# Preparing the keys of the first attention in fixed places of the input block before it

## The chip, the cores and the metric

The kernel runs on one core of one Trainium2 chip. The metric is the device time of one execution in microseconds (us). Beside the times of several runs there is one profiled execution with a trace of every instruction. Engines are named as the profile names them: PE multiplies matrices (PEld loads its weights), DVE, ACT and POOL compute on vectors, SP only issues transfers. Each engine takes its own instructions strictly in the order in which they stand in its queue, and waits where an operand is not ready.

## The reference

One encoder layer on a sequence of 512 tokens of width 2048, in float32. What the change touches is the input projection and the start of mixer A:

```python
h = rmsnorm(x, g_mix)
qa, ka, va, qb, kb, vb = split(h @ w_in)
q = axial_rope(rmsnorm(qa, g_q), s) * hd ** -0.5    # 8 heads of 128
k = axial_rope(rmsnorm(ka, g_k), s)                 # 2 heads of 128
p = softmax(q @ k.T);  out_a = p @ va               # all 512 keys
```

Mixer B (dilated windows), the output projection, a SwiGLU layer and a last norm follow; they are the same in both kernels.

## The kernel before

**Products.** Every float32 operand is split into a high and a low part, and a product is three matmuls (`mm3`, lines 242 to 244): high by high, high by low, low by high. For each tile of weights ACT makes the high part (line 295, in the attention stage) and DVE the low part (line 300); line 271 is its load, issued by SP.

**Units.** The program is a list of units, each one weight tile with its matmuls. The input projection has a first chunk of 16 units (keys and values of mixer A, parked in DRAM as `kvA`), three blocks of 56 column units that use seven products in place of eight (`ColBlock`, products m1 to m7, in the order of `CHAIN`, m3 last), and then two plain chunks of 16 units (`in_plain`), whose units have 12 matmuls each. The queries of mixer A, `qA0` and `qA1`, are made in the first of the three blocks and parked in DRAM too. The last of the three blocks, `last`, is where the change is; its results (the first queries and keys of mixer B) are evicted by lines 939 and 944.

**Pieces between units.** After the matmuls of unit n the program runs the functions hooked to n. `last.after("m3", k, f)` hooks f to the unit k places behind the last m3 unit of the block, so -4 is four units before its end. Besides, `side` is a queue of small pieces of attention work. `give` hands out a credit, 2.8 for each unit in the attention stage (half of it in the middle of the unit, half at its end), and runs pieces from the front of `side` while the credit covers their cost; a piece costs 1 unless `weighed`, `light` or `both` gives it another cost. So neither a clock nor readiness sets the order: it is written out when the program is built, and an engine that comes to a piece whose operand is late stands still, with everything queued behind it.

**The start of the attention.** `load_consts` loads the gains and the rotary tables `ctab`. `reload("kvA", kA)` brings the keys and values back from DRAM, 1 MB in one transfer. `table_tasks` makes six pieces: three for the keys' tables `gsk` and `gck` (lines 420 and 414) and three for the queries' `gsq`, `gcq`. Then, for each of four row tiles t: `scale_k` (ACT, line 501) with the squares of the keys (ACT, line 435, tile `rj`); `split_vA` (ACT line 497, DVE line 498); the squares of the queries with the turned and scaled keys (DVE, lines 448 to 458); the turned and scaled queries (DVE, the same lines on `qA`). A norm's root is taken on POOL after a small DVE instruction (line 222). The keys are transposed by PE (line 506), the queries of the first head by `heads[0].tq` (line 550), which needs all four scaled row tiles; then the slots of the heads begin.

The queue and its start are:

```python
todo = attention_tasks()
last.after("m3", 0, lambda: side.extend(todo))
last.after("m3", 1, lambda: reload("kvA", kA))
last.after("m3", 2, lambda: reload("qA0", qA[0]))
```

Of the kernel before, what the change touches and what calls it, by code (L numbers as in the profile page):

```python
# [23 lines left out]
NT = S // P  # L24
KD = D // P
NC = D // 512
NHA, NKV, NHB = 8, 2, 8
# [42 lines left out]
def encoder_block(ctx, tc, x, g_mix, w_in, g_q_a, g_k_a, g_out_a, g_out_b, w_out, g_ffn,  # L70
# [15 lines left out]
    def slot(base, dtype=F32, shape=(P, 512)):  # L86
        return sp.tile(list(shape), dtype, tag="s", name=nm(base))
# [11 lines left out]
    def bank():  # L99
        return banks.popleft()  # L100

    def release(*tiles):
        banks.extend(tiles)
# [203 lines left out]
    side = deque()  # L307
# [154 lines left out]
    qA, kA, kTA, vA = {}, {}, {}, {}  # L462
# [21 lines left out]
    def reload(name, dst):  # L484
        assert stored[name] == NT, name
        whole = slot(name, F32, (P, NT, 512))
        nc.sync.dma_start(whole, spill[name].rearrange("t p c -> p t c"))
        dst.update((t, whole[:, t]) for t in range(NT))
        dst["whole"] = whole
# [10 lines left out]
    def scale_k(t):  # L500
        nc.scalar.activation(kA[t][:, :256], kA[t][:, :256], AF.Copy, scale=r1["r"][:, t:t + 1])

    def transpose_k_a(kv):
        ps = bank()
        for t in range(NT):
            nc.tensor.transpose(ps[:, t * P:(t + 1) * P], kA[t][:, 256 + kv * HD:256 + (kv + 1) * HD], ident)
        kTA[kv] = split(ps, "kT", at=((2, 4 + 2 * kv), (2, 5 + 2 * kv)))
        release(ps)
# [8 lines left out]
    def split_vB(h):  # L517
        vB[h] = split(vB[h].rearrange("p t c -> p (t c)"), "v", at=heads[NHA + h].home("v"))
# [16 lines left out]
    heads = []  # L535
# [102 lines left out]
    def push_heads():  # L638
        for n in range(2 * NHA):
            heads.append(Head("AB"[n // NHA], n % NHA))  # L640
# [20 lines left out]
    def weighed(cost, f):  # L661
        f.cost = cost
        return f

    def light(cost, tasks):
        return [weighed(cost, f) for f in tasks]

    def attention_tasks():
        def q_tasks(j):
            return norm_rope(lambda t: (qA[j][t], qA[j][t]), 4, "q")  # L670

        def both(cost, *lists):
            return [weighed(cost, lambda fs=fs: [f() for f in fs]) for fs in zip(*lists)]

        qA.update({j: {} for j in range(2)})
        qkB.update({j: {} for j in range(4)})
        push_heads()
        k_squares, k_turned, k_scaled = norm_rope(lambda t: (kA[t][:, :256], kA[t][:, 256:]), NKV, "k")
        q_squares, q_turned, q_scaled = q_tasks(0)
        vs = [lambda t=t: split_vA(t) for t in range(NT)]  # L680
        tables = light(0.8, table_tasks())
        todo = tables[:3] + both(1.4, [lambda t=t: scale_k(t) for t in range(NT)], k_squares)
        todo += both(0.6, vs) + tables[3:]
        todo += both(2.0, q_squares, k_turned, k_scaled) + both(2.6, q_turned, q_scaled)
        todo += light(0.6, [lambda kv=kv: transpose_k_a(kv) for kv in range(NKV)]) + [heads[0].tq, heads[0].tk]
        todo += light(0.1, [lambda: reload("qA1", qA[1])])
        extra = {}

        def at(slot, tasks):
            extra.setdefault(slot, []).extend(tasks)  # L690
        at(20, light(0.1, [lambda: nc.sync.dma_start(mask, c_mask)]))
        q_squares, q_turned, q_scaled = q_tasks(1)
        for t in range(NT):
            at(t // 2, both(0.8, q_squares[t:t + 1]))
            at(2 + 2 * t, both(0.9, q_turned[t:t + 1]))
            at(3 + 2 * t, both(0.9, q_scaled[t:t + 1]))
        for j in range(4):
            s = NT * (NHA + 2 * j)
            at(s - 11, light(0.1, [lambda j=j: reload(f"qkB{j}", qkB[j])]))
            at(s - 7, light(0.9, [lambda j=j: rope_partial(qkB[j]["whole"])]))  # L700
        for h in range(NHB):
            s = NT * (NHA + h)
            at(s + 2, light(0.1, [lambda h=h: load_vB(h)]))
            at(s + 4, light(0.4, [lambda h=h: split_vB(h)]))
        for s in range(2 * NHA * NT + VALUE_LAG + 2):
            cost = 1.5 if s < NHA * NT else 1.2 if s < 2 * NHA * NT else 0.7
            todo += [weighed(cost, lambda s=s: head_slot(s))] + extra.get(s, [])
        return todo

    share = {"now": -1, "credit": 0.0, "due": 1.0}  # L710

# [251 lines left out]
    blocks, ends = [], []  # L963
# [7 lines left out]
              (("qkB2", "qkB3"), heads_b[2:])]  # L971
    for names, lo in groups[:COLUMN_BLOCKS]:
        in_block(names, lo)
    last = blocks[-1]
    last.after("m7", 1, lambda: nc.gpsimd.dma_start(arena[0][:, 1], ar_dram))
    last.after("m3", -2, load_consts)
    todo = attention_tasks()
    last.after("m3", 0, lambda: side.extend(todo))
    last.after("m3", 0, twins.clear)
    last.after("m3", 0, leave_homes)  # L980
    last.after("m5", 0, lambda: fewer_homes("more"))
    last.after("m3", 1, lambda: reload("kvA", kA))
    last.after("m3", 2, lambda: reload("qA0", qA[0]))
    attend = [len(units)]
    for names, lo in groups[COLUMN_BLOCKS:]:
# [508 lines left out]
```

## Time and profile before

| what | value |
|---|---|
| time, median of 3 runs | 1978.44 us (1978.35 to 1980.0) |
| the profiled execution, its own time | 1978.67 us |
| its span in the trace | 1976.9 us |
| PE busy | 1965.3 us |
| DVE busy | 1590.2 us |
| ACT busy | 1130.4 us |

A row of the timeline has the start in us from the span's start, the length, the engine, the line, the operation and its tiles, and how often it stands in a row; in brackets the idle time of the engine before it and what ended that. A length holds the pipeline's fill, so the time that an instruction costs its engine in a row of them is the distance between two starts, a little less than its length. A row of the windows has a stretch of the span, its length, the busy time of PE, PEld, DVE, ACT and POOL in it with their instructions, PE's granted clock (1.00 is full), the share of the transfer engines and GB/s.

### The profile page before, as it was taken

How to read it: one execution, taken by the hardware profiler on the slowest of the kernel's cores; microseconds unless marked ns; L12 is line 12 of the kernel's file. 1: busy time of each engine (PE TensorE's matmuls, PEld its weight loads, DVE VectorE, ACT ScalarE, POOL GpSimd, SP SyncE). 2: the span in 40 equal slices, each digit the busy share in tenths (PEclk: the TensorE clock that was granted, in tenths of full speed). 3: DMA queues.
4: the chain of work that ended last, by engine and by line, in shares of the span. 5: the costliest groups of instructions: out<-in, count | busy, mean ns of one | idle time of the engine just before them, and what ended most of it. 6: DMA issues, size and time to landing. Idle time of an engine off the chain costs nothing.

```text
span 1976.9 us, 27536 instructions
## 1 busy us (share of the span) xinstructions
PE 1965.3 (99%) x8972; PEld 1621.9 (82%) x8972; DVE 1590.2 (80%) x2725; ACT 1130.4 (57%) x2071; POOL 120.3 (6%) x162
## 2 busy tenths in 40 slices
PE   9999999999999999999999999999999999999998
PEld 7888888888888888888888888888888888888886
DVE  6888668888775698887878877878779888878877
ACT  7655555565455565554554555555555666656655
POOL 0100001000000000000000000000000121111121
PEclk9999999999999999999999999999999999999999
DMA  8576683143343564745837747558467698879865
GB/s 279 181 282 205 216 275 126 68 144 128 118 146 104 203 208 163 280 159 193 303 115 253 243 134 279 197 179 287 142 218 267 191 275 252 226 149 264 239 128 171
DMA packets 235873, 394.83 MB, mean 200 GB/s; under 512 B 22560, under 2 KB 77648, under 8 KB 235600
## 3 DMA queue, kind: packets, MB, share of 16 engines
q1 hardware_dynamic: 211440, 330.85, 50.1%
q0 software_dynamic: 17200, 40.38, 9.4%
q10 hardware_dynamic: 7088, 21.83, 3.3%
q8 instruction: 70, 1.15, 0.2%
q14 instruction: 75, 0.61, 0.1%
HBM read 330.33 MB, written 62.65 MB: 199 GB/s over the span
## 4 chain that ended last, share of the span: by engine, by line
PE 95%; DVE 2%; DMA 1%; ACT 1%; issue 1%; SPq 0%; ACTq 0%; POOLq 0%; POOL 0%; DVEq 0%
PE b L242 31%; PE b L244 31%; PE b L243 30%; PE b L600 1%; PE b L1164 1%; DMA raw<-in_w_in_dram 1%; PE b L1088 0%; PE b L326 0%; PE b L550 0%; DVE w L300 0%; ACT rj L435 0%; DVE ra L448 0%; DMA stage<-in_w_in_dram 0%; PE b L561 0%; DVE qA L457 0%
## 5 line engine op out<-in xcount | busy, mean ns | idle before, releaser
L242 PE MATMUL b<-tw,arena 128*128 128x512 f32 x2244 | 879.3, 392 | 0.0
L244 PE MATMUL b<-tw,arena 128*128 128x512 f32 x2244 | 874.1, 390 | 0.0
L243 PE MATMUL b<-tw,arena 128*128 128x512 f32 x2244 | 873.6, 389 | 0.3 <-DVE tw L300 0.3
L828 ACT ACTIVATE tw<-raw 128x512 fp32r<-128x512 f32 x924 | 557.4, 628 | 427.3 <-DVE raw L891 290.9
L831 DVE TENSOR_TENSOR tw<-raw,tw 128x512 fp32r<-128x512 f32 x924 | 619.8, 686 | 161.9 <-ACT tw L828 155.9
L244 PEld LDWEIGHTS b<-tw,arena 128*128 128x128 f32 x2244 | 421.2, 188 | 88.2
L243 PEld LDWEIGHTS b<-tw,arena 128*128 128x128 f32 x2244 | 421.5, 188 | 86.7 <-DVE tw L300 0.6
L242 PEld LDWEIGHTS b<-tw,arena 128*128 128x128 f32 x2244 | 421.4, 188 | 86.3 <-ACT ev L1236 0.7
L891 DVE TENSOR_TENSOR raw<-raw,raw 128x512 f32<-128x512 f32 x528 | 360.3, 683 | 0.7 <-DMA raw<-in_w_gate_up_dram 0.6
L1237 POOL DMA_DIRECT2D x1d<-ev x76 | 66.3, 963 | 1143.9 <-ACT ev L1236 1123.3
L828 ACT ACTIVATE tw<-stage 128x512 fp32r<-128x512 f32 x140 | 85.4, 629 | 67.6 <-DVE stage L891 45.1
L831 DVE TENSOR_TENSOR tw<-stage,tw 128x512 fp32r<-128x512 f32 x140 | 93.3, 685 | 23.5 <-ACT tw L828 23.5
L242 PE MATMUL b<-w,arena 128*128 128x512 f32 x240 | 95.8, 399 | 0.0
L233 ACT ACTIVATE pTh<-b 128x512 fp32r<-128x512 f32 x64 | 38.3, 598 | 100.2 <-PE b L600 96.3
L244 PE MATMUL b<-w,arena 128*128 128x512 f32 x240 | 93.9, 391 | 0.0
L243 PE MATMUL b<-w,arena 128*128 128x512 f32 x240 | 93.5, 390 | 0.0
L1236 ACT ACTIVATE ev<-b,smalls 128x512 f32<-128x512 f32 x76 | 49.7, 683 | 29.0 <-PE b L244 25.8
L365 DVE TENSOR_TENSOR pair<-pair 128x256 f32<-128x256 f32 x120 | 45.5, 421 | 23.6 <-ACT pair L1091 22.6
L1139 DVE TENSOR_TENSOR s<-b,s 128x512 f32<-128x512 f32 x66 | 44.0, 687 | 24.8 <-PE b L244 24.8
L1167 ACT ACTIVATE pair<-b 128x512 f32<-128x512 f32 x44 | 26.3, 598 | 49.6 <-PE b L1164 49.2
L244 PEld LDWEIGHTS b<-w,arena 128*128 128x128 f32 x240 | 45.0, 188 | 10.0
L243 PEld LDWEIGHTS b<-w,arena 128*128 128x128 f32 x240 | 45.2, 188 | 9.1
(210 smaller groups left out, 1797.3 us busy)
## 6 DMA issues: line engine op xcount, KB each, us to landing
raw<-in_w_gate_up_dram SPq DMA_DIRECT2D x616, 256.0 KB, 5.4
raw<-in_w_down_dram SPq DMA_DIRECT2D x176, 256.0 KB, 6.1
stage<-in_w_in_dram SPq DMA_DIRECT2D x111, 256.0 KB, 5.2
forms<-pair SPq DMA_DIRECT2D x22, 896.0 KB, 5.3
x1d<-ev POOLq DMA_DIRECT2D x76, 256.0 KB, 6.8
fr<-forms ACTq DMA_DIRECT2D x35, 512.0 KB, 5.2
raw<-in_w_out_dram SPq DMA_DIRECT2D x32, 512.0 KB, 4.5
stage<-in_w_in_dram SPq DMA_DIRECT2D x90, 128.0 KB, 3.4
```

The source lines that it names most:

```text
L233: nc.scalar.activation(hi, src, AF.Copy)
L242: nc.tensor.matmul(dst, ah, bh, start=start, stop=False, skip_group_check=chained)
L243: nc.tensor.matmul(dst, ah, bl, start=False, stop=False, skip_group_check=chained)
L244: nc.tensor.matmul(dst, al, bh, start=False, stop=stop, skip_group_check=chained)
L365: nc.vector.tensor_tensor(out, x, y, op=op)
L828: nc.scalar.activation(self.pair[:, 0], self.src, AF.Copy)
L831: nc.vector.tensor_tensor(self.pair[:, 1], self.src, f32(self.pair[:, 0]), op=OP.subtract)
L891: nc.vector.tensor_tensor(t[dst], t[src[0]], t[src[1]], op=OP.add if form == "m6" else OP.subtract)
L1139: nc.vector.tensor_tensor(d[:, t], box.bank_of(form)[t], d[:, t], op=OP.add)
L1167: nc.scalar.activation(st["pair"][:, half * 1024:half * 1024 + 512], ps, AF.Copy)
L1236: nc.scalar.activation(e, box.bank_of(form)[t], AF.Copy, scale=r2["r"][:, row:row + 1])
L1237: nc.gpsimd.dma_start(x1_dram[2 * cb + j, row], e, accum_op=OP.add)
```

## The change

The front of the queue becomes a list of its own, `keys`: the three pieces of the keys' tables and the four pieces with `scale_k` and the squares of the keys. They run at fixed units of the last block, the tables and the first row tile after unit -4, the other row tiles after -3, -2 and -1. The constants are loaded at -7 (it was -2) and the reload of the keys at -6 (it was +1). The rest of the queue begins at unit 0 as before, but now with `split_vA`. The list is built at -5, not when the program starts, so that its tables get their place in memory there. The first head's turn, `heads[0].tq`, costs 3 where it cost 1. The reload of the queries stays at +2.

```diff
-        todo = tables[:3] + both(1.4, [lambda t=t: scale_k(t) for t in range(NT)], k_squares)
-        todo += both(0.6, vs) + tables[3:]
+        keys = tables[:3] + both(1.4, [lambda t=t: scale_k(t) for t in range(NT)], k_squares)
+        todo = both(0.6, vs) + tables[3:]
         todo += both(2.0, q_squares, k_turned, k_scaled) + both(2.6, q_turned, q_scaled)
-        todo += light(0.6, [lambda kv=kv: transpose_k_a(kv) for kv in range(NKV)]) + [heads[0].tq, heads[0].tk]
+        todo += light(0.6, [lambda kv=kv: transpose_k_a(kv) for kv in range(NKV)]) + light(3.0, [lambda: heads[0].tq()]) + [heads[0].tk]
...
-        return todo
+        return keys, todo
...
-    last = blocks[-1]
+    last, prepared = blocks[-1], []
     last.after("m7", 1, lambda: nc.gpsimd.dma_start(arena[0][:, 1], ar_dram))
-    last.after("m3", -2, load_consts)
-    todo = attention_tasks()
-    last.after("m3", 0, lambda: side.extend(todo))
+    last.after("m3", -7, load_consts)
+    last.after("m3", -6, lambda: reload("kvA", kA))
+    last.after("m3", -5, lambda: prepared.extend(attention_tasks()))
+    for n in range(7):
+        last.after("m3", (-4, -4, -4, -4, -3, -2, -1)[n], lambda n=n: prepared[0][n]())
+    last.after("m3", 0, lambda: side.extend(prepared[1]))
...
-    last.after("m3", 1, lambda: reload("kvA", kA))
```

What it moves shows best in the order of three engines. On SP, the transfers from the last constants to the reload of the queries; `raw` are the weights of the plain chunks, two transfers for two units. Before:

```order
L208 DMA fixed<-in_c_partial_dram 128x256
L271 DMA raw_2382<-in_w_in_dram 128x2x256 x2
L271 DMA raw_2407<-in_w_in_dram 128x2x256 x2
L271 DMA raw_2410<-in_w_in_dram 128x2x256 x2
L487 DMA kvA_2428<-kvA 128x4x512
L271 DMA raw_2431<-in_w_in_dram 128x2x256 x2
L487 DMA qA_31_2457<-qA_97 128x4x512
```

and now:

```order
L208 DMA fixed<-in_c_partial_dram 128x256
L487 DMA kvA_2340<-kvA 128x4x512
L271 DMA raw_2401<-in_w_in_dram 128x2x256 x2
L271 DMA raw_2432<-in_w_in_dram 128x2x256 x2
L271 DMA raw_2435<-in_w_in_dram 128x2x256 x2
L271 DMA raw_2459<-in_w_in_dram 128x2x256 x2
L487 DMA qA_33_2480<-qA_97 128x4x512
```

The reload of the keys passed three pairs of weight loads; the constants and the reload of the queries stand where they stood.

On ACT, around the end of the block; `ends` are the block's last two evictions, `w` the high parts of the weights of the plain chunk. Before:

```order
L295 ACTIVATE w_2350<-raw_2254 128x512
L295 ACTIVATE w_2366<-raw_2275 128x512
L295 ACTIVATE w_2391<-raw_2275 128x512
L939 ACTIVATE ends_737<-b_76,smalls 128x512
L469 DMA qkB_102<-ends_737 128x512
L939 ACTIVATE ends_737<-b_77,smalls 128x512
L469 DMA qkB_102<-ends_737 128x512
L295 ACTIVATE w_2434<-raw_2382 128x512
L501 ACTIVATE kvA_2428<-kvA_2428,smalls 128x256
L435 ACTIVATE rj_2444,smalls<-kvA_2428 128x128 x2
```

and now:

```order
L295 ACTIVATE w_2387<-raw_2271 128x512
L501 ACTIVATE kvA_2340<-kvA_2340,smalls 128x256
L435 ACTIVATE rj_2398,smalls<-kvA_2340 128x128 x2
L501 ACTIVATE kvA_2340<-kvA_2340,smalls 128x256
L435 ACTIVATE rj_2411,smalls<-kvA_2340 128x128 x2
L295 ACTIVATE w_2416<-raw_2271 128x512
L939 ACTIVATE ends_733<-b_76,smalls 128x512
L469 DMA qkB_102<-ends_733 128x512
L939 ACTIVATE ends_733<-b_77,smalls 128x512
L469 DMA qkB_102<-ends_733 128x512
L497 ACTIVATE arena_86<-kvA_2340,smalls 128x256 x4
L295 ACTIVATE w_2462<-raw_2401 128x512
```

All four scalings and squares of the keys, and two weight splits between them, now stand ahead of the evictions; the split of the values (line 497) follows right behind these.

On DVE, the end of the run of table, key and query pieces, up to the last scaled query tile. Before:

```order
L458 TENSOR_TENSOR qA_31_2457<-qA_31_2457,smalls 128x512
L300 TENSOR_TENSOR w_2635<-raw_2431,w_2634 128x512
L448 TENSOR_TENSOR ra_2680<-qA_31_2457,gsq_118 128x8x32 x2
L451 TENSOR_TENSOR qA_31_2457<-qA_31_2457,gcq_117 128x512
L457 TENSOR_TENSOR qA_31_2457<-qA_31_2457,ra_2680 128x512
L458 TENSOR_TENSOR qA_31_2457<-qA_31_2457,smalls 128x512
L300 TENSOR_TENSOR w_2666<-raw_2489,w_2665 128x512
L448 TENSOR_TENSOR ra_2702<-qA_31_2457,gsq_118 128x8x32 x2
L451 TENSOR_TENSOR qA_31_2457<-qA_31_2457,gcq_117 128x512
L457 TENSOR_TENSOR qA_31_2457<-qA_31_2457,ra_2702 128x512
L458 TENSOR_TENSOR qA_31_2457<-qA_31_2457,smalls 128x512
```

and now:

```order
L458 TENSOR_TENSOR qA_33_2480<-qA_33_2480,smalls 128x512
L300 TENSOR_TENSOR w_2606<-raw_2435,w_2605 128x512
L448 TENSOR_TENSOR ra_2639<-qA_33_2480,gsq_2357 128x8x32 x2
L451 TENSOR_TENSOR qA_33_2480<-qA_33_2480,gcq_2356 128x512
L457 TENSOR_TENSOR qA_33_2480<-qA_33_2480,ra_2639 128x512
L458 TENSOR_TENSOR qA_33_2480<-qA_33_2480,smalls 128x512
L448 TENSOR_TENSOR ra_2651<-qA_33_2480,gsq_2357 128x8x32 x2
L451 TENSOR_TENSOR qA_33_2480<-qA_33_2480,gcq_2356 128x512
L457 TENSOR_TENSOR qA_33_2480<-qA_33_2480,ra_2651 128x512
L458 TENSOR_TENSOR qA_33_2480<-qA_33_2480,smalls 128x512
L300 TENSOR_TENSOR w_2631<-raw_2459,w_2630 128x512
```

One weight split fewer stands ahead of the last query tile. On PE nothing is added or left out; the transposes of the keys stand behind 102 matmuls of the plain chunk (138 before), and those of the first head's queries behind 114 (144 before).

## The prediction, made before the changed kernel was run

> **What bounds the kernel now.** I read the page's busy times first, then the windows around the place of the change, then the timeline of each engine there. The page says that PE is never far from busy:
>
> ```profile
> span 1976.9 us, 27536 instructions
> PE 1965.3 (99%) x8972; PEld 1621.9 (82%) x8972; DVE 1590.2 (80%) x2725; ACT 1130.4 (57%) x2071; POOL 120.3 (6%) x162
> ```
>
> Only 11.6 us of the span are idle on PE in all. Windows show how little of that lies where the change can reach, from the end of the input block to the end of the attention:
>
> ```profile
> 285.00:295.00 10.00, 10.00 (x46) 8.29 (x45) 2.98 (x8) 8.00 (x27) 0.80 (x1) 1.00 0.64 212
> 295.00:325.00 30.00, 29.48 (x139) 24.29 (x138) 28.17 (x63) 12.31 (x47) 3.96 (x2) 1.00 0.43 137
> 335.00:340.00 5.00, 4.86 (x24) 3.50 (x23) 4.83 (x11) 3.97 (x9) 3.65 (x5) 1.00 0.67 238
> 345.00:350.00 5.00, 4.92 (x24) 3.86 (x23) 4.89 (x12) 2.90 (x7) 0.00 (x0) 1.00 0.33 105
> 440.00:460.00 20.00, 19.85 (x103) 16.04 (x103) 18.79 (x44) 13.95 (x29) 0.00 (x0) 1.00 0.12 40
> 600.00:700.00 100.00, 99.78 (x477) 82.24 (x476) 62.95 (x104) 57.61 (x103) 1.04 (x1) 1.00 0.45 150
> ```
>
> The idle times are 0.52, 0.14, 0.08, 0.15 and 0.22 us, 1.11 us together. DVE is nearly idle from 285 to 295 (2.98 of 10 us) and full from 295 to 325 (28.17 of 30). The largest hole of PE belongs to that full stretch; PE's own timeline shows it:
>
> ```profile
> 315.73 0.39 PE L242 MATMUL b<-w,arena 128*128 128x512 f32 x1
> ...
> 317.54 0.39 PE L244 MATMUL b<-w,arena 128*128 128x512 f32 x1
> 317.77 1.03 PE L506 MATMUL b<-fixed,kvA 128*128 128x128 f32 x8
> ...
> 320.03 0.49 PE L550 MATMUL b<-fixed,qA 128*128 128x128 f32 x3
> 321.04 0.33 PE L550 MATMUL b<-fixed,qA 128*128 128x128 f32 x1 [0.52 <-DVE qA L458]
> ```
>
> Three of the first head's four transposes ran at 320.03, and the fourth waited for the last scaled query tile on DVE. Three in 0.49 us with a last length of 0.27 make a pitch of 0.11, so it would have started at 320.36: 0.68 us are lost here (0.52 as idle, the rest inside modelled lengths). Eight matmuls lie between 315.73 and 317.54, a pitch of 0.226 us. So the end is set by PE, and what can change it is how DVE's chain meets PE at this turn.
>
> **The change part by part.** *Fixed pieces at the end of the block.* The work is the same; only places move. PE reaches the first turn 30 matmuls earlier (114 and not 144 ahead of it, by the order): 30 x 0.226 = 6.8 us, so the first transpose would start at 313.2 and the fourth at 313.6. DVE must therefore be 6.8 us earlier as well to break even. ACT's and DVE's timelines say how early it can be:
>
> ```profile
> 279.00 2.19 ACT L295 ACTIVATE w<-raw 128x512 fp32r<-128x512 f32 x4 [2.56 <-DVE tw L831]
> 286.01 0.69 ACT L939 ACTIVATE ends<-b,smalls 128x512 f32<-128x512 f32 x1 [4.82 <-PE b L244]
> ...
> 288.25 0.63 ACT L295 ACTIVATE w<-raw 128x512 fp32r<-128x512 f32 x1 [0.40 <-DMA raw<-in_w_in_dram]
> 288.79 0.49 ACT L501 ACTIVATE kvA<-kvA,smalls 128x256 f32<-128x256 f32 x1
> ...
> 289.92 0.49 ACT L501 ACTIVATE kvA<-kvA,smalls 128x256 f32<-128x256 f32 x1
> ...
> 292.17 0.61 ACT L295 ACTIVATE w<-raw 128x512 fp32r<-128x512 f32 x1
> 292.69 0.49 ACT L501 ACTIVATE kvA<-kvA,smalls 128x256 f32<-128x256 f32 x1
> ...
> 293.82 0.89 ACT L497 ACTIVATE arena<-kvA,smalls 128x256 fp32r<-128x256 f32 x2
> ...
> 296.46 0.30 ACT L435 ACTIVATE rj<-qA 128x128 f32<-128x128 f32 x1
> ...
> 297.63 0.62 ACT L295 ACTIVATE w<-raw 128x512 fp32r<-128x512 f32 x1
> ```
>
> ```profile
> 276.48 2.49 DVE L831 TENSOR_TENSOR tw<-stage,tw 128x512 fp32r<-128x512 f32 x4
> ...
> 293.94 0.17 DVE L222 TENSOR_SCALAR smalls<-smalls 128x8 f32<-128x8 f32 x1 [4.33 <-ACT rj L435]
> 294.34 0.89 DVE L498 SCALAR_TENSOR_TENSOR arena<-kvA,smalls,arena 128x256 fp32r<-128x256 f32 x2 [0.23 <-ACT arena L497]
> ...
> 300.40 0.69 DVE L300 TENSOR_TENSOR w<-raw,w 128x512 fp32r<-128x512 f32 x1
> 301.01 0.49 DVE L448 TENSOR_TENSOR ra<-kvA,gsk 128x128 f32<-128x128 f32 x2
> ...
> 305.78 0.17 DVE L222 TENSOR_SCALAR smalls<-smalls 128x16 f32<-128x16 f32 x1
> ...
> 320.30 0.69 DVE L458 TENSOR_TENSOR qA<-qA,smalls 128x512 f32<-128x512 f32 x1
> ```
>
> DVE waited 4.33 us for the keys' squares, then ran without a break from the first value split (294.34) to the end of the last scaled query (320.99): 26.65 us. Eight weight splits (0.61 each, 300.40 to 301.01) lie in that run before, seven in the new order, so it takes 26.04 us now. It cannot begin before ACT has made the first value split, and that stands behind the block's two evictions, which wait for PE's last matmuls (286.01, after 4.82 us of idle). If ACT comes to them on time, it is free of both at 288.25, makes the value split in 0.52 (293.82 to 294.34), and DVE runs from 288.77 to 314.81. PE wants the tile at 313.6 and has it 0.05 later than DVE's end, as before (320.99 to 321.04): a wait of 1.3 us where 0.68 stood.
>
> *Where ACT's hole is filled.* One key tile costs ACT 1.13 us (288.79 to 289.92), a weight split 0.52 (292.17 to 292.69). Ahead of the evictions stand four tiles and two of the four splits that ran at 279: 4 x 1.13 + 2 x 0.52 = 5.56 us. They end by 286.01 if the keys are back by 280.45. The hole of 4.82 us hides nearly all of it; without the hole the whole 5.56 would fall on the chain.
>
> *The reload.* Its time decides, and it was never issued at that place. SP's own rows and the transfers' landing times bound it:
>
> ```profile
> 271.05 0.33 SPq L208 DMA_DIRECT2D fixed<-in_c_partial_dram  x1
> 272.62 5.36 SPq L271 DMA_DIRECT2D raw<-in_w_in_dram  x6
> 278.99 0.37 SPq L487 DMA_DIRECT2D kvA<-kvA  x1
> ...
> 290.03 0.37 SPq L487 DMA_DIRECT2D qA<-qA  x1
> ```
>
> ```profile
> 270.00:280.00 10.00, 10.00 (x46) 8.29 (x45) 6.80 (x12) 5.12 (x10) 1.08 (x2) 1.00 0.96 302
> 280.00:285.00 5.00, 5.00 (x24) 4.14 (x23) 2.20 (x6) 1.19 (x3) 0.00 (x0) 1.00 1.06 395
> ...
> raw<-in_w_in_dram SPq DMA_DIRECT2D x28, 256.0 KB, 6.4
> qA<-qA SPq DMA_DIRECT2D x2, 1024.0 KB, 5.8
> ...
> kvA<-kvA SPq DMA_DIRECT2D x1, 1024.0 KB, 8.2
> ```
>
> It stands right behind the last constant, so it is issued between 271.4 (that one's end) and 272.6 (where the next transfer went before). With its own 8.2 us it lands from 279.6 to 280.8. The engines were full in that stretch (0.96, 302 GB/s), and a pair of weight loads follows at once: 0.5 MB more at 302 GB/s are 1.7 us, so the upper bound is 282.5. Below 279.6 nothing speaks for it. I take 281.5, nearer the upper end, since the constants ahead of it are not yet through when it is issued. ACT is then late by 1.05, DVE ends at 315.9, and PE waits 2.35. [...]
>
> *The three weight pairs that the reload passed* serve units 4 to 9 of the plain chunk. The first keeps its place but for the reload's own issue (0.37). The second, of units 6 and 7, now waits for DVE's last column split (276.48 + 2.49 = 278.97), for which the reload waited before. The chunk starts at 317.77 - 138 x 0.226 = 286.6, its unit 6 at 286.6 + 6 x 12 x 0.226 = 302.9; 279.0 plus 8.2 leaves 15 us. Cost nothing; the cover is gone only past 300.
>
> *The reload of the queries* waits for the buffer of the last keys' squares (281.5 + 4 x 1.13 + 0.52 = 286.5, not 290.03). With 5.8 it lands at 292.3, just as ACT comes to the queries' squares. These take 4 x 1.17 (296.46 to 297.63) and two splits, 5.7 us, to 298.0. DVE needs them for line 222, which stands 15.21 us ahead of the run's end (305.78 to 320.99), so at 300.7 now. Covered by 2.7 us; a landing past 295 would cost one for one.
>
> *The late evictions.* If ACT is 1.05 late, so are they; the next that PE writes into their banks is the first head's turn, at 313. Nothing.
>
> *Tables and constants.* The constants stay at their place on SP, since the loads around them were written at the same points. The keys' tables run in DVE's idle time before 286 as before. The list built at -5 issues nothing. Nothing.
>
> *The turn that costs 3.* It gives one unit, twelve matmuls, between the key transposes and the first turn where six stood. Those six matmuls (1.36 us) are inside the 114; at cost 1 the wait would be 3.7.
>
> *Everything after* comes two to three units earlier relative to the weights; no instruction of PE is more or less. Its remaining holes after 325 were 0.59 us in sum. The plain chunk's evictions no longer coincide with the next head's turn, so I count the 0.14 at 335 as gone and keep the rest.
>
> **Sum.** Profiled execution 1978.67, plus 2.35 - 0.68 = 1.67, minus 0.14: 1980.2. The profiled execution stands 0.23 above the median of the runs shown, so the forecast for the median is 1980.0 us, 1.5 us slower than before. A measurement of this kernel can tell about 0.2%, 4 us, from no change; the forecast is no change by that.
>
> **The rivals.** (1) *The reload is on time.* It lands by 280.45; the wait is 1.3, the time 1978.9. For it: its own row, 8.2 us, with the earliest issue. Against: the constants in front of it are not through yet.
>
> (2) *Slower: the reload is the new bound.* One mechanism: the keys land late, ACT stands at line 501 with weight splits, evictions and value split behind it, and the turn pays one for one. From a landing at 284.0 on the loss is over 4 us. If the reload and the pair behind it are served like two transfers of 1 MB in a row, 8.2 + 3.5 us (1 MB at 302 GB/s) after 272.6, the landing is 284.3, ACT late by 3.9, the wait 5.2, the time 1982.8. For it: 0.96 share. Against: the row of 8.2 was taken at an even fuller moment (1.06 from 280 to 285).
>
> [...]
>
> (3) *A gain.* DVE's run shrinks more than by one split, or the later holes close as well: all of 1.11 us of idle and the 0.16 hidden at the turn go, 1978.44 - 1.3 = 1977.1. Against: the value split is tied to PE's last matmuls, and the run from there is 26 us long whatever is moved ahead.
>
> (4) *The change does not do what it says.* Were a piece still where it was, the time would be 1978.4. The order shows the reload, the scalings and squares moved; only the constants did not.
>
> **How the numbers follow.** The forecast (keys between 280.5 and 283) 0.58, on time 0.16, slower by the reload 0.15, a gain 0.07, nothing done 0.02, other stalls 0.02. The range leaves out the far ends: low 1977.5, between the gain and no change; high 1983.0, above the case of the late reload without the clock. Slower by over 0.2% (above 1982.4): the late reload and an unknown stall, 0.16. Faster by over 0.2% (below 1974.5): no mechanism offers 4 us where only 1.3 are idle, 0.03. Within: 0.81.
>
> **What would show it.** Right: the reload issued at 271 to 273 and the first scaling on ACT near 281.5; evictions at 286 to 287.1; DVE's first value split at 288.8 to 289.9, its last scaled query ending at 314.8 to 315.9; an idle time of 1.2 to 2.3 us on PE before line 550, ended by DVE. Wrong: a hole of PE at a weight split of units 2 to 11, a wait of line 222 for the queries' squares, a first scaling after 284, or no wait at the turn at all.

## The result, and the profile after

| | median us | runs | profiled execution, span |
|---|---|---|---|
| before | 1978.74 | 6 (1978.35 to 1980.0) | 1978.67, 1976.9 |
| changed | 1986.46 | 6 (1982.48 to 1987.91) | 1982.48, 1980.7 |

The ratio is 1.0035, 95% interval 1.0025 to 1.0045: 7.7 us slower. The forecast was 1980.0, from 1977.5 to 1983.0, so the time lies outside. The profiled execution of the changed kernel is also its shortest one; what the trace shows is the lower end of the loss, 3.8 us. The page of the changed kernel:

```profile
span 1980.7 us, 27547 instructions
PE 1965.4 (99%) x8972; PEld 1622.4 (82%) x8972; DVE 1590.8 (80%) x2725; ACT 1130.3 (57%) x2071; POOL 121.2 (6%) x162
```

PE's work is the same to 0.1 us; only idle time was added. The view of waits names it (engine and line that waited, what released it, us in total, times, longest):

```profile
PE b L550 <- DVE qA L458: 1.5, 1, 1.5
...
PE b L242 <- DVE smalls L580: 1.2, 1, 1.2
PE b L242 <- DVE pTl L234: 1.1, 1, 1.1
PE b L600 <- DVE pTl L234: 1.0, 2, 0.7
```

The windows say where (the changed kernel, columns as before):

```profile
285.00:295.00 10.00, 10.00 (x46) 8.29 (x45) 6.14 (x17) 8.14 (x32) 2.06 (x1) 1.00 0.85 286
295.00:325.00 30.00, 28.47 (x134) 23.40 (x134) 26.91 (x56) 13.12 (x52) 3.07 (x1) 1.00 0.32 108
...
340.00:345.00 5.00, 3.94 (x20) 2.95 (x18) 4.89 (x11) 4.01 (x9) 1.09 (x2) 1.00 0.76 262
...
415.00:420.00 5.00, 4.29 (x22) 3.28 (x21) 4.74 (x11) 2.40 (x5) 0.00 (x0) 1.00 0.03 13
440.00:460.00 20.00, 18.57 (x94) 14.72 (x93) 17.59 (x41) 12.99 (x28) 0.00 (x0) 1.00 0.22 78
600.00:700.00 100.00, 99.78 (x470) 82.20 (x469) 61.28 (x103) 54.66 (x96) 1.42 (x1) 1.00 0.47 160
```

Idle are 1.53 us at the turn, 1.06 at 341, 0.71 at 418, 1.43 at 447 and 0.22 later, 4.95 together where 1.11 stood before. That is the 3.8 us between the two spans. Only 1.0 of them is at the turn.

At the turn the chain ran as the prediction laid it out. The timelines of SP, ACT, DVE and PE of the changed kernel:

```profile
272.39 0.91 SPq L487 DMA_DIRECT2D kvA<-kvA  x1
```

```profile
281.16 0.51 ACT L501 ACTIVATE kvA<-kvA,smalls 128x256 f32<-128x256 f32 x1 [0.61 <-DMA kvA<-kvA]
...
286.74 0.67 ACT L939 ACTIVATE ends<-b,smalls 128x512 f32<-128x512 f32 x1
...
289.02 1.71 ACT L497 ACTIVATE arena<-kvA,smalls 128x256 fp32r<-128x256 f32 x4 [0.40 <-ACT ends L939]
```

```profile
289.56 0.48 DVE L498 SCALAR_TENSOR_TENSOR arena<-kvA,smalls,arena 128x256 fp32r<-128x256 f32 x1 [2.45 <-ACT arena L497]
...
314.92 0.69 DVE L458 TENSOR_TENSOR qA<-qA,smalls 128x512 f32<-128x512 f32 x1
```

```profile
313.65 0.49 PE L550 MATMUL b<-fixed,qA 128*128 128x128 f32 x3
315.67 0.33 PE L550 MATMUL b<-fixed,qA 128*128 128x128 f32 x1 [1.53 <-DVE qA L458]
```

The keys were there at 281.1, ACT came to the evictions at 286.74, DVE's run went from 289.56 to 315.61, and PE stood 1.53 us. That is 1.69 us of lost time where 0.68 stood before (the fourth transpose could have started 0.33 behind 313.65), so 1.01 more; the sum had 1.67. So the question is the three holes behind the turn, and why five of six executions took 2.9 to 5.4 us more than the traced one.

### The profile page after: what moved, and what is told of

Its sections match the earlier page's. It is cut to its first block, busy times and chain, and to the rows that moved or that the text cites. A ratio compares the mean times of both kernels' runs of the same rounds, so it can differ in the third digit from the quotient of the medians.

```text
span 1980.7 us, 27547 instructions
## 1 busy us (share of the span) xinstructions
PE 1965.4 (99%) x8972; PEld 1622.4 (82%) x8972; DVE 1590.8 (80%) x2725; ACT 1130.3 (57%) x2071; POOL 121.2 (6%) x162
## 4 chain that ended last, share of the span: by engine, by line
PE 93%; DVE 3%; DMA 2%; issue 1%; ACT 1%; SPq 0%; ACTq 0%; POOLq 0%; DVEq 0%; POOL 0%
PE b L242 30%; PE b L244 30%; PE b L243 30%; PE b L600 1%; PE b L1166 1%; DMA raw<-in_w_in_dram 1%; DVE tw L831 0%; DVE w L300 0%; PE b L1090 0%; PE b L326 0%; DVE ra L448 0%; PE b L550 0%; SPq L271 0%; DMA stage<-in_w_in_dram 0%; DMA raw<-in_w_out_dram 0%
```

## The experiments

Two edits serve many runs. The kernel's memory is full, and a moved queue changes how long tiles live, so nearly every variant needs some of it. *Five buffers* takes one of six from the pairs of weight loads; *own buffers* gives the tiles of the evictions of line 478 a ring of four, so that no other tile is laid over them:

```diff
-RAWS = {"raw": 6, ...}
+RAWS = {"raw": 5, ...}
```
```diff
-            e = homes.popleft() if name == "kvA" else slot("ev" + name)
+            e = homes.popleft() if name == "kvA" else sp.tile([P, 512], F32, tag="evq", bufs=4, name=nm("ev" + name))
```

Five buffers have all runs below but the changed kernel with own buffers, the reload at -9, turn 1 and the turn's cost alone, which keep six, and two that say four. In code, `...` stands for what is not shown.

What the traces of all runs show, in us; "turn" is PE's wait at line 550 (with the 0.2 just behind it where only the slots are early), or (w) at a weight split just behind the last scaled query; "half" is the number of stretches of half clock; waits elsewhere, none over 0.7, are left out:

| run | median (before beside it) | turn | 338 to 352 | 418 | 445 to 455 | near 1702 | half |
|---|---|---|---|---|---|---|---|
| before | 1978.74 | 0.52 | 0.08 (at 346) | - | 0.15 | - | 0 |
| changed | 1986.46 (1978.74) | 1.53 | 1.06 | 0.71 | 1.43 | - | 0 |
| five buffers | 1985.99 (1978.93) | 2.52 | 1.05 | 0.71 | 1.08 | - | 0 |
| pause | 1985.00 (1978.93) | 2.61 | 1.09 | - | 0.15 | 1.90 | 2 |
| turn 9 | 1984.92 (1978.93) | 0.84 w | 1.01 | - | 0.14 | 0.90 | 0 |
| before, slots early | 1990.72 (1978.93) | 0.76 | 3.25 | 0.71 | 2.72 | 1.54 | 1 |
| before, five buffers | 1979.04 (1978.97) | 0.53 | - | - | 0.11 | - | 0 |
| turn 9, own buffers | 1983.38 (1978.97) | 2.80 w | 0.71 | - | 0.15 | 0.75 | 1 |
| changed, own buffers | 1984.86 (1978.97) | 2.84 | 1.07 | 0.71 | 0.24 | - | 2 |
| pause, own buffers | 1984.54 (1978.97) | 1.75 | 0.53 | - | 0.13 | 2.06 | 0 |
| reload at -9 | 1987.99 (1978.68) | 2.74 | 1.10 | 0.71 | 1.38 | 1.40 | 1 |
| before, slots early, own buffers | 1984.39 (1978.68) | 0.74 | 2.53 | 0.71 | 0.24 | - | 0 |
| three out | 1985.32 (1978.68) | 3.10 w | 1.13 | - | 0.13 | 0.52 | 1 |
| turn 1 | 1988.80 (1978.68) | 3.99 | 0.61 | - | 3.39 | - | 3 |
| keys alone | 1979.46 (1978.94) | 0 | 0.71 | - | 0.16 | 1.67 | 0 |
| reload alone | 1980.88 (1978.94) | 0.54 | 0.44 | - | 0.13 | 1.25 | 0 |
| turn 3 alone | 1982.02 (1978.94) | 0 | 1.83 | - | 0.79 | 1.27 | 0 |
| keys alone, four buffers | 1982.19 (1978.67) | 1.36 | 2.90 | - | 0.14 | - | 0 |
| keys alone, other places | 1978.62 (1978.98) | 0 | 0.76 | - | 0.14 | - | 0 |

**Controls.** The changed kernel and the kernel before, each with five buffers; the order on every engine stays.

> The changed kernel with five buffers in place of six for the pairs of weight loads, nothing else; every engine's order of instructions stays the same. It is the control of the other runs, which need that memory. Both theories: 1985 to 1988 us, 6 to 9 above the kernel before, with idle times of PE near 340, 417 and 446 us of 1.1, 0.7 and 1.2. If the buffer matters, a wait of the transfer queue for it would show ahead of line 271 and the time would be over 1989.

1985.99 us, ratio 1.0034 (1.0021 to 1.0046), as the changed kernel. The wait at the turn was 2.52 in this trace although the keys landed early, at 280.73: DVE's line 420 stood 1.29 us for the transfer of `ends`, in whose place the queries' table lay here.

> The kernel before with five buffers in place of six for the pairs of weight loads; the order on every engine is that of before. Control for the other runs with five, three of which had a late wait near 1700 us (line 242 on the evictions of line 1236 or 1238, 0.9 to 1.9 us) that neither the kernel before nor the changed one shows. If the fifth buffer is innocent: 1978.3 to 1979.5 us and no such wait. If it causes that wait: 1980 to 1983, with the wait.

1979.04 us, ratio 1.0000 (0.9991 to 1.0009), no wait near 1700. The missing buffer costs nothing by itself.

**Pause: only the first turn early.**

```diff
-        todo += light(0.1, [lambda: reload("qA1", qA[1])])
+        todo += light(6.1, [lambda: reload("qA1", qA[1])])
```

> The changed kernel, but the reload of the second queries costs 6.1 in place of 0.1: keys, reload and the first head's turn stay early (30 matmuls ahead of before), everything from the first head's keys on is back at its old place against the weights. Theory A (the loss comes from the rest of the queue running 24 to 48 matmuls early): the wait at the turn stays at 1.5 us, the idle times at 340, 417 and 446 are gone, 1979 to 1981 us. Theory B (the loss comes from the early keys and their reload, or from the clock after the wait at the turn): 1985 to 1988.

1985.00 us, ratio 1.0039. The holes at 418 and 447 went, as theory A says, but the time is B's. The turn now cost 2.61, and a stretch of half clock lay behind it (the granted clock was 0.97 from 280 to 340 us, 1.00 in the changed kernel), by an estimate from that mean up to 1.8 more (0.03 of 60 us); 1.09 stood at 352, where ACT's line 587 waited 2.4 us for the transfer of an eviction.

**Turn 9: turn and slots at their old places.**

```diff
-        ... + light(3.0, [lambda: heads[0].tq()]) + ...
+        ... + light(9.0, [lambda: heads[0].tq()]) + ...
```

> The changed kernel, but the first head's turn costs 9 in place of 3: the keys and their reload stay early, the turn and everything behind it are back at their old places against the weights, to the matmul. Theory A (rest of the queue early): no wait at the turn, no idle times behind it, 1977.5 to 1979.5 us. Theory B (early keys and reload themselves): 1983 to 1988. Theory C (the wait at the turn, and a lower clock behind it): 1977.5 to 1979.5 too, but then the run with the later slots alone at their old places stays at 1985.

1984.92 us, ratio 1.0031 (1.0019 to 1.0042). No wait at line 550, none at 418 and 447, and still 6 us slow. The run of DVE that ends with the last scaled query was pulled forward, and the weight splits of the units stand behind it in DVE's order: PE waited 0.84 at such a split. Theories A and C fall as they were put. B's range holds the time, but the wait stands behind the pulled run and not at the keys, so the keys alone had to be asked (below). In front of the 1.01 at 347 line 587 again waited for an eviction's transfer, 2.2 us.

**Before, slots early: only the rest of the queue forward.**

```diff
-            cost = 1.5 if s < NHA * NT else ...
+            cost = 1.0 if s < 12 else 1.5 if s < NHA * NT else ...
```

> The kernel before, but the first twelve slots of the heads cost 1.0 in place of 1.5, which takes the same 6 credits out of the queue: keys, reload and the first turn stay as they were, and from the 13th slot on everything stands exactly where the changed kernel has it against the weights (24 to 48 matmuls early). Theory A: the idle times near 417 and 446 come back, 1981.5 to 1987 us, with the lower clock too if that belongs to them. Theories B and C: 1978 to 1979.5, as before.

1990.72 us, ratio 1.0060 (1.0048 to 1.0073): with keys, reload and turn untouched, the advance of the slots alone costs more than the whole change. The 0.71 near 418 is back, in the same instruction as in the changed kernel.

**Own buffers.** Four of these orders again with the evictions' tiles apart.

> As the run with the turn at 9, same order on every engine, but the tiles of the plain chunks' evictions (line 478) take four buffers of their own, so that no tile of the softmax is laid over one that is still on its way to DRAM. Theory D (the program's order is the same as before behind the turn, and what costs is a buffer: line 587 waits 2.2 us for the transfer of an eviction, PE 1.0 at 347): that wait and the idle time at 347 go, what stays is 0.84 at line 300 near 316, 1979 to 1982 us. Theory B (early keys and their reload by themselves): as the run with the turn at 9, 1983 to 1987.

1983.38 us, ratio 1.0023, in B's range and not in D's. No tile waited any more for the transfer of an eviction of line 478, and the hole at 350 fell from 1.01 to 0.71 only; so theory D holds for the wait and explains less than a third of the hole. The keys landed 2.0 us later than with shared buffers (282.79 and 280.74), and the wait at the weight split was 2.80.

> The changed kernel, same order on every engine and six buffers for the weight loads, but with four buffers of their own for the tiles of the evictions of line 478. Theory D: the wait of line 234 for an eviction's transfer (1.1 us) and the idle time of PE at 447 (1.2) go; the idle times that belong to the order stay: 1.5 to 2.5 at the turn, 1.06 at 341, 0.71 at 418. 1981 to 1985 us. Theory A (the order alone): all idle times stay, 1985 to 1988.

1984.86 us, ratio 1.0026 (1.0017 to 1.0035). The hole at 447 went and only its 0.24 stayed. How it arose in the changed kernel: DVE's line 234 waited for the transfer of an eviction whose buffer it was to fill, DVE then ran without a break to line 580, and PE stood there. DVE's timeline, then PE's:

```profile
442.40 0.69 DVE L234 TENSOR_TENSOR pTl<-b,pTh 128x512 fp32r<-128x512 f32 x1 [1.13 <-DMA qkB<-evqkB]
447.00 0.68 DVE L580 CUSTOM_DVE_ANT_0 p<-b,mask 128x512 f32<-128x512 f32 x1
```

```profile
447.74 0.51 PE L242 MATMUL b<-kTh,qTh 128*128 128x512 f32 x1 [1.19 <-DVE smalls L580]
```

The holes at the turn, at 341 and at 418 stayed to 0.01 us or grew; they are not the buffers'.

> As the run with the pause of 6 credits behind the first turn, same order on every engine, with four buffers of their own for the tiles of the evictions of line 478. Only the first turn is early here. Theory D: the wait of line 587 for an eviction's transfer (2.4 us) and the idle time at 352 (1.1) go, the wait at the turn (1.5 to 2.5) stays; where the clock is halved for one stretch of 3.4 us behind it, 1.7 more: 1979.5 to 1984 us. Theory B: 1984.5 to 1988.

1984.54 us, ratio 1.0027, at B's lower edge. The wait of line 587 went and the hole near 350 halved (1.09 to 0.53); 1.75 at the turn and a new 2.06 near 1702 stayed.

> As the kernel before with its first twelve slots at 1.0, same order on every engine, with four buffers of their own for the tiles of the evictions of line 478. Keys, reload and the first turn are as before; only the rest of the queue is early. Theory A and D together: the 3.2 us at 346 and most of the 1.8 at 454 belonged to transfers of evictions and go; about 1.0 near 341 and 0.71 near 423 belong to the order and stay: 1980 to 1984 us. Theory A alone: 1988 to 1992 as in that run.

1984.39 us, ratio 1.0030 (1.0018 to 1.0041), against 1990.72 with shared buffers. Own buffers took 2.5 us out near 450 and 0.9 at 346, where all 3.2 were expected to go; 2.36 there and 0.71 at 420 remain without that transfer. PE's timeline of this run:

```profile
420.42 0.66 PE L600 MATMUL b<-fixed,p 128*128 128x128 f32 x4 [0.71 <-DVE pTl L234]
```

Six traces, the changed kernel's among them, have the slots at these places, and all six show 0.71; the other thirteen show none.

**The reload three units earlier.**

```diff
-    last.after("m3", -6, lambda: reload("kvA", kA))
+    last.after("m3", -9, lambda: reload("kvA", kA))
```

> The changed kernel with the reload of the keys three units earlier (-9 in place of -6), ahead of the constants; the order on PE, ACT, DVE and POOL stays the same. Theory R (the wait at the turn and its spread between executions come from when the keys land): they land before 280.5 us, line 501 doesn't wait for them, the wait at the turn is the 1.2 to 1.5 that the value split sets, no stretch of half clock follows it, and what stays is 341, 418 and 447: 1981 to 1983.5 us. If the landing does not matter: 1985 to 1988 as the changed kernel. If the constants, now behind 1 MB, are late: DVE waits at line 420 and the turn pays.

1987.99 us, ratio 1.0046. Line 501 waited for nothing, and yet DVE's value split started at 291.25 and the turn cost 2.74: the weight splits of DVE and ACT waited 5.6 and 2.1 us for the transfer of `ends`, whose places they had got, so the tables and evictions were late instead. Theory R is not confirmed; the landing is one of several things that the start of the chain waits for.

**All three suspects out.** Reload at -9, turn at 5, the queries' reload at 4.1, own buffers, four buffers for the pairs.

```diff
-        ... + light(3.0, [lambda: heads[0].tq()]) + ...
+        ... + light(5.0, [lambda: heads[0].tq()]) + ...
-        todo += light(0.1, [lambda: reload("qA1", qA[1])])
+        todo += light(4.1, [lambda: reload("qA1", qA[1])])
...
```

> The changed kernel with all three suspects taken out: the reload of the keys at -9, the turn at cost 5 and the reload of the second queries at 4.1 (so that the turn is 18 matmuls early in place of 30 and the slots are where they were before), the evictions of line 478 in four buffers of their own, and four buffers for the pairs of weight loads to make room. If reload, advance of the queue and buffers are the whole loss: no wait over 0.6 us between 290 and 600, 1977.5 to 1980.5 us. If the early keys cost by themselves: 1983 or more.

1985.32 us, ratio 1.0031. It failed as an experiment: the queries' reload waited 5.1 us on SP for the transfer of `ends`, in whose place it now lay, was issued at 287.62, and ACT waited for it until 296.45:

```profile
296.45 0.31 ACT L435 ACTIVATE rj<-qA 128x128 f32<-128x128 f32 x1 [5.51 <-DMA qA<-qA]
```

It told nothing on the early keys, and the next runs ask that again.

**Turn 1.**

```diff
-        ... + light(3.0, [lambda: heads[0].tq()]) + ...
+        ... + light(1.0, [lambda: heads[0].tq()]) + ...
```

> The changed kernel with the first head's turn at cost 1, as before the change, so the turn comes 6 matmuls (1.4 us) sooner and the rest of the queue some more. The prediction gave 1.4 us more of wait for it: 2.7 to 4.2 at the turn. If PE's clock is halved for one or two stretches of 3.4 us when more than half of such a stretch is idle, every execution gets it: a stretch at 0.5 in the trace right behind the turn, 1986 to 1991 us. If the clock takes no part: 1983.5 to 1987, no such stretch.

1988.80 us, ratio 1.0049. The turn waits 1.48 + 2.52 (the second is DVE's time for one more query tile), two stretches of half clock follow at once and a third behind 445: right behind the turn matmuls start 0.43 us apart (317.46 to 317.89), where the kernel before has 0.226, and the mean granted clock of this execution is 0.997, against 0.999 in the trace of the changed kernel. The clock takes part.

**The keys alone.** The full change, but the first value split waits for 8 credits and the turn costs 1, so PE's order is that of before to the matmul; own buffers, five buffers.

```diff
-        todo = both(0.6, vs) + tables[3:]
+        todo = both(8.6, vs[:1]) + both(0.6, vs[1:]) + tables[3:]
```

> The changed kernel with the first value split at cost 8.6 in place of 0.6 and the turn back at 1: from the first value split on, every matmul of PE stands where it stood before the change (PE's order is that of before), and only the keys' tables, scalings, squares and their reload are early. Own buffers for the evictions of line 478, five for the pairs of weight loads. Theory A (the loss comes from what was pulled forward behind the keys: value splits, queries, turn and slots): DVE's run starts no later than before, no new wait of PE, 1977.5 to 1979.5 us. Theory B (early keys or their reload cost by themselves): 1982 or more.

1979.46 us, ratio 1.0003 (0.9994 to 1.0012). The early keys and their early reload cost nothing that can be measured. Theory B falls.

**The reload alone** (the kernel before, `load_consts` at -7 and the reload at -6, own buffers, five buffers).

> The kernel before with the constants at -7 and the reload of the keys at -6, nothing else of the change; PE's, ACT's and DVE's orders are those of before. Own buffers for the evictions of line 478, five for the pairs of weight loads. Theory A: the transfer ahead of the weight pairs costs nothing by itself, 1978 to 1979.5 us. Theory B: weights of the first units late, a wait of PE at a split in units 2 to 11, 1981 or more.

1980.88 us, ratio 1.0013 (1.0004 to 1.0022). No wait at any weight split of units 2 to 11. Of the 1.9 us, 1.25 stand near 1700 and 0.36 near 347; neither is where the reload could act, so the transfer itself is not shown to cost. The time lies between the two ranges.

**The turn's cost alone** (the kernel before with the turn at 3, own buffers).

> The kernel before with the first head's turn at cost 3, nothing else of the change, and own buffers for the evictions of line 478. The turn is 6 matmuls later, the slots 6 to 12, so the wait of 0.52 at the turn goes: 1977.8 to 1979 us if no new one comes. If any move of the slots against the evictions makes DVE late (theory A in its widest form: the old places are a narrow optimum), a wait near 341 to 352 or 418 to 455 comes instead: 1980 to 1984.

1982.02 us, ratio 1.0015 (1.0006 to 1.0024). The 0.52 at the turn went, and 1.83 at 349 and 0.79 at 453 to 455 came.

**The keys alone, other places.** Twice the same order on PE, ACT, DVE and POOL: with four buffers for the pairs, and with five but without own buffers.

> As the run with the keys alone early (PE, ACT, DVE and POOL in the same order), but with four buffers for the pairs of weight loads in place of five, which lays the down projection's loads over tiles as in the kernel before: the load that was issued 17 us late near 1630 there gets its old place. If the 1.67 us at 1700 come from that load, they go, and with no wait at the turn the time is 1976.8 to 1978.7, at or a little below the kernel before. If they don't, 1979 to 1980 as that run.

1982.19 us, ratio 1.0018. The wait near 1700 went, but with four buffers the queries' reload was issued at 288.16 and ACT waited 3.24 for it: 1.36 at the turn and 1.45 behind it.

> As the first run with the keys alone early, same order on every engine and five buffers for the pairs of weight loads, but without own buffers for the evictions of line 478: only the places of tiles differ. No load of the down projection lies over a tile that is freed just ahead of it, as one does in that run. If the 1.67 us at 1700 belong to places of buffers they go, and with the queries' reload on time (five buffers, not four) there is no wait at the turn: 1977 to 1979 us, even with the kernel before or a little below. If the early keys cost by themselves, 1980 or more.

1978.62 us, ratio 1.0000 (0.9991 to 1.0009). Even with the kernel before; no version that was run is faster than the kernel before. PE's timeline of this run:

```profile
319.94 0.60 PE L550 MATMUL b<-fixed,qA 128*128 128x128 f32 x4
...
345.68 0.50 PE L242 MATMUL b<-pTh,arena 128*128 128x512 f32 x1 [0.76 <-DVE pTl L234]
```

The turn waits no longer, and 0.76 stand at 346 where the kernel before had 0.08: what was won at one meeting of PE and DVE was given back at the next.

## Why the prediction was wrong

**The reload, ACT's hole, DVE's run, the turn: right.** Landing 281.1 (281.5 was taken, between 280.5 and 282.5), evictions 286.74 (286 to 287.1), value split 289.56 (288.8 to 289.9), end of the last scaled query 315.61 (314.8 to 315.9), idle at the turn 1.53 (1.2 to 2.3). The wait varies, and not with the landing alone: in three traces with the changed order the same transfer took 8.2, 8.8 and 10.5 us and PE waited 2.52, 1.53 and 2.84. The earliest landing, in the run with five buffers, goes with a wait of 2.52, for there a tile lay over `ends`. The prediction's bounds for the landing were 279.6 and 282.5; measured were 280.7, 281.1 and 282.7, the last just past the upper one.

**The weight pairs, the queries' reload, the late evictions, tables and constants: nothing, as said.** PE did not wait at a split of units 2 to 11, and line 222 of the queries, at 300.39, did not wait. With the turn at 1 PE waited 3.99 there, against 1.53 to 2.84 in the traces with 3; the prediction had 3.7.

**The step that failed** is the last: "Everything after comes two to three units earlier relative to the weights; no instruction of PE is more or less. ... The plain chunk's evictions no longer coincide with the next head's turn, so I count the 0.14 at 335 as gone and keep the rest." The 0.14 did go. The rest did not keep: holes of 0.45 us in sum became 3.42, so that behind the turn 2.8 us were added in the trace where the sum had 0.14 taken away. The argument counted PE's instructions and left out that the work of DVE and ACT between two meetings with PE changes when the slots move against the units. Two runs show that the loss comes from what moved behind the keys and not from the keys: the keys alone early cost nothing (1978.62 against 1978.98), the slots alone early 5.7 with own buffers (1984.39 against 1978.68). The parts do not add up to shares: with the slots back and the turn early 5.6 remained (pause, own buffers), with the turn back too 4.4 (turn 9, own buffers); in both the run of DVE up to the last scaled query is still early. The traced execution of 1982.48 lies inside the forecast's range by luck: it holds these 2.8 us, which the sum did not have.

A part of the hole at 341 can be read off DVE's groups of lines. From the end of the last scaled query to the end of the `pTl` for which PE waits, DVE needs 25.34 us before (320.99 to 346.33) and 26.02 now (315.61 to 341.63). The groups of line 300 in that stretch, before and then now:

```profile
L300 DVE TENSOR_TENSOR w<-raw,w 128x512 fp32r<-128x512 f32 x7 | 4.8, 683 | 0.0
```

```profile
L300 DVE TENSOR_TENSOR w<-raw,w 128x512 fp32r<-128x512 f32 x8 | 5.5, 684 | 0.0
```

One weight split more, 0.7 us; every other group has the same count. PE needs only 24.96 us from the turn to the place where it stands (315.67 to 340.63), so it stands 1.06. That place is not the one of before. PE's timeline, before and then now:

```profile
345.02 0.39 PE L242 MATMUL b<-arena,qTh 128*128 128x512 f32 x1
...
345.71 0.60 PE L600 MATMUL b<-fixed,p 128*128 128x128 f32 x4
346.38 0.50 PE L242 MATMUL b<-pTh,arena 128*128 128x512 f32 x1
```

```profile
341.69 0.50 PE L242 MATMUL b<-arena,qTh 128*128 128x512 f32 x1 [1.06 <-DVE pTl L234]
...
342.49 0.60 PE L600 MATMUL b<-fixed,p 128*128 128x128 f32 x4
342.85 0.48 PE L242 MATMUL b<-pTh,arena 128*128 128x512 f32 x1
```

Before, a score (`qTh`) and four transposes ran while `pTl` was not ready yet, and PE met DVE only at the product that uses it. Now the score itself waits. It does not read `pTl`; what it can need of that instruction is only the bank `b` that line 234 reads, for the program takes its eight banks of matmul results in turn (`bank()`, `release()`). From the score's start to that product 1.16 us pass, so by this estimate most of the 1.06 would be covered if the score had another bank. The holes at 418 (line 600, which reads `p`) and at 447 (line 242, which reads keys and queries) have the same form. No run changed the banks, so this is read off the rows and not tested.

That this stretch is DVE's and not PE's the prediction could have seen: before, PE met DVE there with 0.08 of idle, the same near-tie as at the turn, and the run with the keys alone shows that 0.5 won at the turn comes back as 0.76 there. The rivals had no such case, only a chance of 0.02 for other stalls; (2) had PE wait for a late engine, but at the turn alone.

**Buffers.** 1.2 us at 447 came from a tile laid over an eviction on its way to DRAM. The prediction did not consider that moved lifetimes change which tiles share a place.

**The clock.** The upper end of the prediction's range, 1983.0, was set without the clock, and nothing in its sum stands for it; the runs show what it added. The windows of the changed kernel with own buffers, cut into stretches of 3.41 us (third value from the right: the granted clock):

```profile
313.20:316.61 3.41, 1.28 (x7) 0.68 (x5) 3.27 (x7) 0.00 (x0) 0.00 (x0) 1.00 0.00 0
316.61:320.03 3.42, 2.70 (x7) 2.22 (x8) 3.42 (x6) 1.12 (x2) 0.00 (x0) 0.50 0.65 160
320.03:323.44 3.41, 3.41 (x9) 2.64 (x9) 0.84 (x2) 0.00 (x0) 0.00 (x0) 0.50 0.83 300
323.44:326.85 3.41, 3.41 (x18) 2.82 (x18) 1.56 (x3) 2.17 (x10) 0.00 (x0) 1.00 0.00 0
```

And of the kernel before with early slots and own buffers:

```profile
343.61:347.02 3.41, 1.68 (x7) 1.42 (x8) 3.34 (x7) 1.26 (x3) 0.00 (x0) 1.00 0.00 0
347.02:350.43 3.41, 3.41 (x18) 2.83 (x17) 3.34 (x9) 1.54 (x4) 0.00 (x0) 1.00 0.06 8
```

In the first, 2.13 us of idle in one stretch were followed by two stretches at 0.50 (9 matmuls in a full one where 18 ran at 1.00, 1.7 us lost by this estimate); the first of them had 0.72 us of idle itself, the second none, and then the clock was back at 1.00. In the second, 1.73 us of idle were followed by 1.00; the rest of that wait, 0.64 us, lay ahead of these rows. With shared buffers and the same slots 3.16 us were idle from 343.02 to 346.43; the clock was 0.50 from there to 349.85, with 9 matmuls, and 1.00 behind that. In the changed kernel the 1.53 us at the turn lay between 313.20 and 316.61, and the clock was 1.00 there and behind it, so that a wait of 1.53 cost 1.53. One of 2.52 (five buffers) left it at 1.00 as well, in the windows from 280 to 400, while the 1.90 near 1702 in the run with the pause went with 0.99 from 1600 to 1800. One of 2.84 (own buffers, the first rows above) cost 5.9: 3.05 more by the clock, half of the 2.70 and 3.41 us that PE was busy at 0.50. So the length of a wait alone did not say whether the clock fell.

The spread of the changed kernel, 1982.48 to 1987.91, is explained by this in part only. The mean granted clock of every execution is on record: the traces without a stretch of half clock have 0.998 or 0.999, those with one 0.998, those with two or three 0.997. The changed kernel with six and with five buffers (the same order) took 1982.48, 1983.36, 1983.94 and 1986.06 us at 0.999, 1985.39 to 1987.43 at 0.998, and 1987.43 to 1988.15 at 0.997. So the clock takes part in the longest ones. But 1986.06 is 3.6 us over the traced execution without it, and no trace shows where. In sum, of the 7.7 us the trace shows 3.8: 1.0 at the turn, 1.8 at 341 and 418, and 1.2 at 447 that a buffer explains (less 0.2 of holes that went). The other 3.9 lie in executions without a trace: a later turn and the clock are argued for them from the runs with the same order, not shown.

**What stays open.** Every edit also lays tiles anew, so a difference of under 1 us between two variants can't be put down to its edit alone. Why a slot's advance yields exactly 0.71 at 418 was not taken apart, nor was it tried whether another order of the banks makes the three holes smaller. The turn with an early chain and on-time weight splits was not reached in any run.

## What to carry to other kernels

Taking work off the front of an ordered queue moves everything behind it; each later place where the bounding engine meets an engine that is nearly as full has to be costed, and a near-tie there (0.08 us of idle) is as good as a bound. What the engines share there counts too: here a score stood 1.06 us behind an instruction whose result it does not read, as read off the rows for a bank that both use; no run tested that. A gain at one meeting is only real if the next one has slack. Where tiles share memory, compare after each move which instructions wait for transfers out.

## What the runs showed of the hardware

The granted clock fell from 1.00 to 0.50 and came back: for 6.83 us in the changed kernel with own buffers (316.61 to 323.44), after 2.13 us of idle PE in 3.41, and for 3.42 us in the kernel before with early slots (346.43 to 349.85), after 3.16 us of idle in 3.41. After 1.73 us of idle in 3.41 (the same slots with own buffers) and 1.53 (the changed kernel) it was 1.00.

Two runs that differ in places of memory alone differed 1.4 ms behind the edit. The wait near 1702 stood in ten of the seventeen runs behind the two kernels, and two of the seventeen, one with it and one without, have the same order on every engine: the keys alone with own buffers and with other places. SP's timelines there, the first and then the second, and PE's of the first:

```profile
1628.94 4.38 SPq L271 DMA_DIRECT2D raw<-in_w_down_dram  x8
```

```profile
1611.41 21.26 SPq L271 DMA_DIRECT2D raw<-in_w_down_dram  x5
```

```profile
1700.36 0.50 PE L242 MATMUL b<-tw,arena 128*128 128x512 f32 x1 [1.67 <-ACT ev L1238]
```

The first issues nothing from 1610 to 1628.9, the second issues from 1611.4 on; the first has 1.67 us of idle PE 70 us later, the other none. In nine of the ten traces with this wait SP issues nothing for 22.8 to 26.0 us between two of these loads, in the traces without it for 11.0 at most. The tenth (the turn's cost alone) has 9.4 and waits 1.27, so the late loads are not the only cause, and the way from them to PE was not followed.
